# A two-layer decoder trunk on one core: layer 0's rows at a pitch of 2624 bytes, its split weights displaced by chunk, and its matmuls in series of four chunks

## The chip, the core and the metric

The kernel runs on one core of a Trainium2 chip. The metric is the device time of one execution in microseconds (us); before the change it is 2330.52 us, the median of three runs. The core's engines work side by side, each on its own queue of instructions: TensorE (PE: matmuls; PEld: the loads of their weights), VectorE (DVE), ScalarE (ACT), GpSimd (POOL) and SyncE (SP), which issues most transfers from HBM. Semaphores order them where one needs what another made.

## What is computed

The reference is a decoder trunk for one sequence of 256 tokens behind 16 learned ones, with 2048 features, 16 heads of 128 and two layers. Layer 0 has a causal softmax attention with forget gates, layer 1 a stick-breaking attention on keys and values of their own projection; each layer ends in a squared-ReLU MLP of width 8192. Cut to its core:

```python
h = concatenate([meta, x], axis=1)                     # 272 x 2048
for layer in range(2):
    a = rms_norm(h, norm_attn[layer])
    if layer < 1:
        q, k, v, f_logit = split(a @ fox_w_in[0], ...)
        cum_logf = cumsum(log_sigmoid(f_logit + fox_b_f[0]))
        h = h + forgetting_attention(q, k, v, cum_logf) @ fox_w_o[0]
    else:
        k_s, v_s = split(rms_norm(h, kv_norm) @ w_kv, 2)
        q = a @ sb_w_q[0]
        h = h + stick_breaking_attention(q, k_s, v_s) @ sb_w_o[0]
    h = h + square(relu(rms_norm(h, norm_mlp[layer]) @ w_up[layer])) @ w_down[layer]
return rms_norm(h, final_norm)[:, 16:]
```

All of it is in fp32.

## The kernel before

The residual `hT` stays in SBUF, features on the 128 partitions: 16 chunks of 128 features, each with its 272 tokens in a row. Layer 0 works on all 272 tokens, layer 1 on the 256 behind the learned ones, but for its keys and values, which are made from all 272. In the code, `t0` is 0 for work on 272 tokens and 16 (`M`) for work on 256. What the texts call layer 0's shape is every group with `t0` = 0.

**Products in three parts.** A projection in fp32 is made from matmuls of the faster type fp32r. Each factor is split in a high part and a rest: x in x hi and x lo, the weights in whi and wlo. A product is whi·hi + whi·lo + wlo·hi; the fourth is left out. `Split` (the class above `split_chunk`) gives one tile of the pool `xs` in which each of the 16 chunks has a row of 640 floats (`XROW`, 2560 bytes), with hi and lo in the same row. `ROWS` says where in the row each begins, in floats: (48, 368) with 272 tokens, (0, 304) with 256.

**Groups.** `gemm_group` makes 512 output features, four output tiles `accs[m]` of 128 each, from all 2048 input features: 4 `kb` of 4 chunks `kc`, hence 4 × 4 × 4 × 3 = 192 matmuls. There are 96 groups, in the order of the program: 12 for Q, K and V and 4 for the output projection of layer 0, 32 for its MLP (up, then down, in four slices of 2048 hidden features), then 4 for Q, 8 for K and V, 4 for the output projection and 32 for the MLP of layer 1. For each `kb`, SP loads 4 chunks of raw weights in two halves `hf` of 2 chunks each (512 KB a transfer) into `raw` (pool `wraw`, 4 buffers). ScalarE copies a half to `whi` with rounding (L229), VectorE subtracts to get `wlo` (L230); both lie in the pool `wspl`, with 4 buffers of each. A `whi` tile holds the two chunks of its half at a pitch of 576 floats (2304 bytes) with `t0` = 16, where they begin 16 floats (64 bytes) in, and at a pitch of 512 floats (2048 bytes) with `t0` = 0, where they begin at 0.

**Order of the matmuls.** `gemm_matmul` (L182) issues each and, but for the first group, ties it behind the one before, so that TensorE's order in a group is the one that the loops write. `runs` cuts the 48 matmuls of a `kb`: in `kb` 0 and 3 into quarters by output tile (all four chunks for one `m`), in `kb` 1 and 2 into halves by chunk pairs (two chunks for all four `m`). In the first group's `kb` 0 a run is one chunk, as its data are still arriving. Within a run `series` sets the order: with `t0` = 16 first all whi·hi, then all whi·lo, then all wlo·hi; with `t0` = 0 the three of one chunk behind each other.

```python
rows = rows[:, o:o + NC * XROW].rearrange("p (c t) -> p c t", c=NC)
...
    whi = whi.rearrange("p (k c) -> p k c", k=2)[:, :, 16:528]
...
    whi = whi[:, :1024].rearrange("p (k c) -> p k c", k=2)
...
elif kb in (0, 3):
    runs = [(range(4), [m]) for m in range(4)]
else:
    runs = [(range(2 * hf, 2 * hf + 2), range(4)) for hf in range(2)]
```

**What takes up the sums.** When an output tile's last matmul in `kb` 3 is done, `evac` reads it from PSUM on VectorE. In the MLP's up groups that is `relu` (L495), a square on ScalarE, and the split of the result into the next x (`x_u`); in the down groups it is `residual_add` (L259). The attention has matmuls of its own, among them `pta` (L594 to L596) in layer 1. The end of the kernel scales the residual into `ob`, a tile of the pool `xs` as well.

Of the kernel before, what the change touches and what calls it, by code (L numbers as in the profile page):

```python
# [9 lines left out]
F32 = mybir.dt.float32  # L10
F32R = mybir.dt.float32r
# [4 lines left out]
P = 128  # L16
D = 2048
NC = D // P
M = 16
# [6 lines left out]

ROWS = {0: (48, 368), M: (0, 304)}
SPAN = 6
XROW = 640

G_A0, G_M0, G_KV, G_A1, G_M1, G_FIN = range(6)

# [2 lines left out]
def yoco_kernel(ctx: ExitStack, tc: tile.TileContext, hT_in, gains, b_f, w_f, w_qkv0, w_o0, w_up, w_dn,  # L35
                w_kv, w_q1, w_o1, outT):
    nc = tc.nc
# [5 lines left out]
    wspl = ctx.enter_context(tc.tile_pool(name="wspl", bufs=4))  # L43
    xs = ctx.enter_context(tc.tile_pool(name="xs", bufs=2))
# [70 lines left out]
    pad = align.tile([P, 32], F32, name="pad")  # L115
# [3 lines left out]
    class Split:  # L119


        def __init__(self, label, t0):
            n = T - t0
            self.t0 = t0
            rows = xs.tile([P, NC * XROW + 64], F32R, tag="x", name=f"x_{label}")
            hi, lo = ROWS[t0]
            o = min(hi, lo)
            rows = rows[:, o:o + NC * XROW].rearrange("p (c t) -> p c t", c=NC)
            self.hi, self.lo = (rows[:, :, k - o:k - o + n] for k in (hi, lo))

            if t0:
                self.wide = {}
                for name, k in (("hi", hi), ("lo", lo)):
                    nc.gpsimd.tensor_copy(rows[:, 0, k - o + n:k - o + n + SPAN], pad[:, :SPAN])
                    self.wide[name] = rows[:, 0, k - o:k - o + n + SPAN]

    def split_chunk(sp, gi, c):

# [41 lines left out]
    def gemm_matmul(*args, **kw):  # L180

        ins = nc.tensor.matmul(*args, **kw).ins  # L182
        if queued and pinned[0]:
            tc.add_manual_dep(ins, queued[0].name, mybir.DependencyInfo(mybir.DependencyClass.NoSync,
                                                                        mybir.DependencyReason.DATA))
        queued[:] = [ins]

    def gemm_group(wblk, sp, t0, evac, before={}, after={}, load_x=None, widen=False):

        uid[0] += 1
        u = uid[0]
        accs = [pacc.tile([P, 512], F32, tag="acc", name=f"acc_{u}_{m}") for m in range(4)]
        n = T - t0
        for kb in range(4):
            src_w = wblk[kb].rearrange("p (k c) -> p k c", k=4)
            if kb in before:  # L200
                before[kb]()
            piece = 1 if load_x is not None and kb < 2 else 2
            raws = [wraw.tile([P, 2, 512], F32, tag="raw", name=f"raw_{u}_{kb}_{hf}") for hf in range(2)]
            for k0 in range(0, 4, piece):
                if load_x is not None:
                    load_x(range(4 * kb + k0, 4 * kb + k0 + piece))
                if load_x is not None and kb == k0 == 0:

                    for c0 in (0, 256):
                        nc.scalar.dma_start(raws[0][:, 0, c0:c0 + 256], src_w[:, 0, c0:c0 + 256])  # L210
                else:
                    nc.sync.dma_start(raws[k0 // 2][:, k0 % 2:k0 % 2 + piece], src_w[:, k0:k0 + piece])
            parts = []
            for hf in range(2):
                whi = wspl.tile([P, 2 * 576], F32R, tag="whi", name=f"whi_{u}_{kb}_{hf}")
                wlo = wspl.tile([P, 2, 576], F32R, tag="wlo", name=f"wlo_{u}_{kb}_{hf}")
                if t0:
                    whi = whi.rearrange("p (k c) -> p k c", k=2)[:, :, 16:528]
                    wlo = wlo[:, :, 16:528]
                else:  # L220
                    whi = whi[:, :1024].rearrange("p (k c) -> p k c", k=2)
                    wlo = wlo[:, :, :512]
                boxes = [(o, piece, 0, 512) for o in range(0, 2, piece)]
                if load_x is not None and kb == hf == 0:
                    boxes[:1] = [(0, 1, 0, 256), (0, 1, 256, 512)]
                for o, no, c0, c1 in boxes:
                    src = raws[hf][:, o:o + no, c0:c1]
                    hp, lp = whi[:, o:o + no, c0:c1], wlo[:, o:o + no, c0:c1]
                    on_act = nc.scalar.activation(hp, src, AF.Copy)  # L229
                    on_dve = nc.vector.tensor_tensor(out=lp, in0=src, in1=hp.bitcast(F32), op=ALU.subtract)  # L230
                parts.append((whi, wlo))
            if kb in after:
                with tc.issue_after(on_act.ins), tc.issue_after(on_dve.ins):
                    after[kb]()


            if load_x is not None and kb == 0:
                runs = [([kc], range(4)) for kc in range(4)]
            elif kb in (0, 3):
                runs = [(range(4), [m]) for m in range(4)]  # L240
            else:
                runs = [(range(2 * hf, 2 * hf + 2), range(4)) for hf in range(2)]
            pinned[0] = load_x is None
            for kcs, ms in runs:
                if t0:
                    series = [(w, x, kc, m) for w, x in ((0, "hi"), (0, "lo"), (1, "hi")) for m in ms for kc in kcs]
                else:
                    series = [(w, x, kc, m) for m in ms for kc in kcs for w, x in ((0, "hi"), (0, "lo"), (1, "hi"))]
                for i, (w, x, kc, m) in enumerate(series):
                    over = SPAN if widen and kb == m == 0 and i in (0, 4, 8) else 0  # L250
                    rhs = sp.wide[x] if over else getattr(sp, x)[:, 4 * kb + kc]
                    gemm_matmul(accs[m][:, :n + over], parts[kc // 2][w][:, kc % 2, m * P:(m + 1) * P], rhs,
                                start=kb == kc == w == 0 and x == "hi", stop=kb == kc == 3 and w == 1)
                if kb == 3:
                    for m in ms:
                        evac(m, accs[m][:, :n])
# [9 lines left out]
    def load_x(chunks):  # L266
        c0, n = chunks[0], len(chunks)
        nc.sync.dma_start(hT[:, c0:c0 + n, :], hT_in[:, c0:c0 + n, :])
        if c0 == 0:
            nc.sync.dma_start(g_sb, gains)  # L270
        for c in chunks:
            split_chunk(xa, G_A0, c)
# [86 lines left out]
    for g in range(4):  # L359
# [11 lines left out]
        if g == 0:  # L371

            gemm_group(w_qkv0[0], xa, 0, lambda m, acc, qT=qT: nc.scalar.copy(qT[:, m, :], acc),
                       after={kb: (lambda kb=kb: first_norm(kb)) for kb in range(4)}, load_x=load_x)
            gate_products()
            box["rstd"] = norm.finish()
            for m in range(4):
                evac_q(m, qT[:, m, :])
            forget_gates(box["rstd"])
        else:  # L380
            gemm_group(w_qkv0[3 * g], xa, 0, evac_q)
# [4 lines left out]
        def decays(j):  # L386

            for i, (o, n) in enumerate(((0, 144), (144, T))):
                nc.vector.scalar_tensor_tensor(out=s[:, j, o:o + n], in0=fk[:, j, :n],
                                               scalar=fq_sb[:, i, 4 * g + j:4 * g + j + 1],  # L390
                                               in1=maskA[:, o:o + n], op0=ALU.subtract, op1=ALU.add)

        gemm_group(w_qkv0[3 * g + 1], xa, 0, lambda m, acc: evac_kv(m, acc, kT),
                   after={j: (lambda j=j: decays(j)) for j in range(4)})

# [254 lines left out]
    a, y, t, rs = (fin[:, i, :] for i in range(4))  # L650
# [9 lines left out]
    for i in range(2):  # L660
# [2 lines left out]
            nc.tensor.matmul(pr[:, b * P:(b + 1) * P], rs[:, b:b + 1].to_broadcast([P, P]), ident,  # L663
                             start=True, stop=True)
        prs.append(pr[:, :S])
    ob = xs.tile([P, NC * XROW + 64], F32, tag="x", name="ob")[:, :NC * XROW].rearrange("p (c t) -> p c t", c=NC)
    pr_sb = tmp.tile([P, T], F32, tag="relu", name="pr_sb")[:, :S]
    nc.scalar.copy(pr_sb, prs[1])
    for c, n in [(12, 1), (13, 1), (14, 1), (15, 1), (0, 2), (2, 2), (4, 2), (6, 2)]:
# [62 lines left out]
```

## Time and profile before

| | before |
|---|---|
| median of three runs | 2330.52 us (2330.20 to 2330.76) |
| the profiled execution | 2330.78 us |
| its span, first to last instruction | 2329.0 us |
| mean granted clock of TensorE | 0.998 |
| TensorE busy | 2317.9 us, 19,030 matmuls |
| VectorE busy | 1290.1 us |
| ScalarE busy | 1041.3 us |
| HBM read | 407.29 MB, 176 GB/s over the span |

The profile is that of one execution. Busy time is the union of an engine's instructions; matmuls overlap, so that the duration of one (about 0.28 us) is longer than the distance between the starts of two. The chain of waits goes back from the last instruction to what released it, and gives rows of start, length and count. A row of the timeline has the start in the span, the length from the first start to the last end, the engine, the line, the operation with output and inputs, and the count; what stands in brackets is idle time ahead of it and what ended it. A row that groups instructions ends in busy time and mean duration in ns, then the idle time before them.

### The profile page before, as it was taken

Reading aid. Unit: us, or ns where it says so; the run is one execution under the profiler, and the core shown is the slowest. Engines: PE = TensorE matmul, PEld = TensorE weight load, DVE = VectorE, ACT = ScalarE, POOL = GpSimd, SP = SyncE. Lnnn points to the kernel's source line nnn. Section 1 sums busy time; section 2 is a strip of 40 time slices with the busy share of each in tenths; the row PEclk is TensorE's granted clock in tenths of the full one; section 3 lists DMA queues with packets and bytes.
Section 4 is the critical chain, followed back from the end, with each engine's and each line's share of the span. In section 5 each row is a group of like instructions: output and inputs, shape, how many; then the busy total and the mean of one; then the engine's idle time right before and its main releaser. Section 6 shows DMA issues by size and latency. Waiting matters only on the chain.

```text
span 2329.0 us, 44826 instructions
## 1 busy us (share of the span) xinstructions
PE 2317.9 (100%) x19030; PEld 2310.8 (99%) x19030; DVE 1290.1 (55%) x1764; ACT 1041.3 (45%) x1397; POOL 41.6 (2%) x72
## 2 busy tenths in 40 slices
PE   9999999999999999999999999999999999999998
PEld 9999999999999999999999999999999999999998
DVE  7666556554455455455665555566545555555554
ACT  6444344443343344344544444445534443443543
POOL 1000000000000000000000000000000000000000
PEclk9999999999999999999999999999999999999999
DMA  7544545555555555555555444455565655656563
GB/s 235 170 164 157 180 154 168 185 173 181 181 171 183 172 186 176 181 172 183 172 191 181 158 152 151 151 178 186 184 193 180 196 181 185 196 183 191 178 195 127
DMA packets 116904, 412.32 MB, mean 177 GB/s; under 512 B 13520, under 2 KB 16992, under 8 KB 116704
## 3 DMA queue, kind: packets, MB, share of 16 engines
q1 hardware_dynamic: 114560, 406.29, 53.3%
q8 instruction: 149, 2.44, 0.4%
q10 hardware_dynamic: 2144, 3.17, 0.4%
q14 instruction: 51, 0.42, 0.1%
HBM read 407.29 MB, written 2.11 MB: 176 GB/s over the span
## 4 chain that ended last, share of the span: by engine, by line
PE 99%; DMA 1%; DVE 0%; ACT 0%; SPq 0%; issue 0%; DVEq 0%; ACTq 0%
PE acc L182 95%; DMA raw<-w_qkv 1%; PE ps L401 0%; PE pv L334 0%; PE pza L579 0%; PE po L463 0%; PE po L618 0%; PE pzb L580 0%; PE po L619 0%; PE po L464 0%; DVE ob L674 0%; PE pf L301 0%; PE pf L300 0%; PE pta L594 0%; PE pta L595 0%; PE pp L433 0%
## 5 line engine op out<-in xcount | busy, mean ns | idle before, releaser
L230 DVE TENSOR_TENSOR wlo<-raw,whi 128x1024 fp32r<-128x1024 f32 (+1 forms) x773 | 928.6, 1217 | 761.0 <-ACT whi L229 760.5
L229 ACT ACTIVATE whi<-raw 128x1024 fp32r<-128x1024 f32 (+1 forms) x773 | 797.1, 1050 | 1033.7 <-PE acc L182 1010.5
L182 PE MATMUL acc<-x_m,whi 128*128 128x272 f32 (+1 forms) x4096 | 650.8, 283 | 0.0
L182 PE MATMUL acc<-x_u,whi 128*128 128x272 f32 (+1 forms) x4096 | 650.7, 283 | 0.0
L182 PEld LDWEIGHTS acc<-x_m,whi 128*128 128x128 f32 x4096 | 572.3, 188 | 0.1
L182 PEld LDWEIGHTS acc<-x_u,whi 128*128 128x128 f32 x4096 | 572.0, 188 | 0.0
L182 PE MATMUL acc<-x_u,wlo 128*128 128x272 f32 (+1 forms) x2048 | 445.2, 284 | 0.0
L182 PE MATMUL acc<-x_m,wlo 128*128 128x272 f32 (+1 forms) x2048 | 445.2, 284 | 0.0
L182 PE MATMUL acc<-x_a,whi 128*128 128x272 f32 (+1 forms) x2048 | 361.7, 289 | 0.1
L182 PEld LDWEIGHTS acc<-x_u,wlo 128*128 128x128 f32 x2048 | 327.6, 189 | 0.0
L182 PEld LDWEIGHTS acc<-x_m,wlo 128*128 128x128 f32 x2048 | 327.6, 189 | 0.0
L182 PEld LDWEIGHTS acc<-x_a,whi 128*128 128x128 f32 x2048 | 303.2, 189 | 1.2 <-ACT whi L229 0.3
L182 PE MATMUL acc<-x_a,wlo 128*128 128x272 f32 (+1 forms) x1024 | 254.9, 287 | 0.0
L182 PE MATMUL acc<-x_kv,whi 128*128 128x272 f32 x1024 | 191.8, 288 | 0.0
L182 PEld LDWEIGHTS acc<-x_a,wlo 128*128 128x128 f32 x1024 | 176.6, 189 | 1.1 <-issue 0.5
L182 PE MATMUL acc<-x_o,whi 128*128 128x272 f32 (+1 forms) x1024 | 163.7, 284 | 0.0
L182 PEld LDWEIGHTS acc<-x_kv,whi 128*128 128x128 f32 x1024 | 159.7, 188 | 0.0
L182 PE MATMUL acc<-x_kv,wlo 128*128 128x272 f32 x512 | 147.5, 288 | 0.0
L182 PEld LDWEIGHTS acc<-x_o,whi 128*128 128x128 f32 x1024 | 143.2, 188 | 0.0
L259 DVE TENSOR_TENSOR hT<-acc,hT 128x272 f32<-128x272 f32 (+1 forms) x160 | 69.1, 432 | 88.8 <-PE acc L182 87.7
L182 PE MATMUL acc<-x_o,wlo 128*128 128x272 f32 (+1 forms) x512 | 111.6, 284 | 0.0
L182 PEld LDWEIGHTS acc<-x_kv,wlo 128*128 128x128 f32 x512 | 96.5, 188 | 0.0
(225 smaller groups left out, 973.4 us busy)
## 6 DMA issues: line engine op xcount, KB each, us to landing
raw<-w_up SPq DMA_DIRECT2D x256, 512.0 KB, 4.5
raw<-w_dn SPq DMA_DIRECT2D x256, 512.0 KB, 4.4
raw<-w_qkv SPq DMA_DIRECT2D x92, 512.0 KB, 3.8
raw<-w_o SPq DMA_DIRECT2D x64, 512.0 KB, 4.1
raw<-w_kv SPq DMA_DIRECT2D x64, 512.0 KB, 3.8
raw<-w_q SPq DMA_DIRECT2D x32, 512.0 KB, 4.7
fk<-f_dram ACTq DMA_DIRECT2D x4, 544.0 KB, 5.3
raw<-w_qkv SPq DMA_DIRECT2D x7, 256.0 KB, 4.5
```

Of the source, the lines that this page charges most:

```text
L182: ins = nc.tensor.matmul(*args, **kw).ins
L229: on_act = nc.scalar.activation(hp, src, AF.Copy)
L230: on_dve = nc.vector.tensor_tensor(out=lp, in0=src, in1=hp.bitcast(F32), op=ALU.subtract)
L259: nc.vector.tensor_tensor(out=hT[:, c, t0:], in0=acc, in1=hT[:, c, t0:], op=ALU.add)
```

## The change

For work with `t0` = 0, three things change; with `t0` = 16 the offsets in a row and the order stay as they were.

1. The rows of an x tile are 656 floats apart (2624 bytes) instead of 640. The tile itself becomes 16 × 656 floats for all, and begins with the row, without the earlier shift by the smaller offset. The final `ob` keeps rows of 640 floats in the new tile.
2. A weights tile has 1216 floats. With `t0` = 0 its two chunks are 592 floats (2368 bytes) apart, and the second half of a `kb` begins 32 floats (128 bytes) in: the four chunks of a `kb` begin 0, 64, 128 and 192 bytes past a multiple of 256.
3. `kb` 1 and 2 run in quarters by output tile too (in the first group `kb` 2 alone), and the series is the same for both values of `t0`: four chunks of whi·hi, four of whi·lo, four of wlo·hi.

```diff
-XROW = 640
+XROWS = {0: 656, M: 640}
+XTILE = NC * 656
...
-            rows = xs.tile([P, NC * XROW + 64], F32R, tag="x", name=f"x_{label}")
+            rows = xs.tile([P, XTILE], F32R, tag="x", name=f"x_{label}")
             hi, lo = ROWS[t0]
-            o = min(hi, lo)
-            rows = rows[:, o:o + NC * XROW].rearrange("p (c t) -> p c t", c=NC)
-            self.hi, self.lo = (rows[:, :, k - o:k - o + n] for k in (hi, lo))
+            rows = rows[:, :NC * XROWS[t0]].rearrange("p (c t) -> p c t", c=NC)
+            self.hi, self.lo = (rows[:, :, k:k + n] for k in (hi, lo))
...
-                whi = wspl.tile([P, 2 * 576], F32R, tag="whi", name=f"whi_{u}_{kb}_{hf}")
-                wlo = wspl.tile([P, 2, 576], F32R, tag="wlo", name=f"wlo_{u}_{kb}_{hf}")
-                if t0:
-                    whi = whi.rearrange("p (k c) -> p k c", k=2)[:, :, 16:528]
-                    wlo = wlo[:, :, 16:528]
-                else:
-                    whi = whi[:, :1024].rearrange("p (k c) -> p k c", k=2)
-                    wlo = wlo[:, :, :512]
+                whi, wlo = (wspl.tile([P, 1216], F32R, tag=t, name=f"{t}_{u}_{kb}_{hf}") for t in ("whi", "wlo"))
+                o, pitch = (16, 576) if t0 else (32 * hf, 592)
+                whi, wlo = (w[:, o:o + 2 * pitch].rearrange("p (k c) -> p k c", k=2)[:, :, :512] for w in (whi, wlo))
...
-            elif kb in (0, 3):
+            elif kb in (0, 3) or not t0 and (load_x is None or kb == 2):
                 runs = [(range(4), [m]) for m in range(4)]
...
-                if t0:
-                    series = [(w, x, kc, m) for w, x in ((0, "hi"), (0, "lo"), (1, "hi")) for m in ms for kc in kcs]
-                else:
-                    series = [(w, x, kc, m) for m in ms for kc in kcs for w, x in ((0, "hi"), (0, "lo"), (1, "hi"))]
+                series = [(w, x, kc, m) for w, x in ((0, "hi"), (0, "lo"), (1, "hi")) for m in ms for kc in kcs]
...
-    ob = xs.tile([P, NC * XROW + 64], F32, tag="x", name="ob")[:, :NC * XROW].rearrange("p (c t) -> p c t", c=NC)
+    ob = xs.tile([P, XTILE], F32, tag="x", name="ob")[:, :NC * 640].rearrange("p (c t) -> p c t", c=NC)
```

More of the change, by code (lines that the diff above doesn't have):

```diff
@@ L133, in __init__ @@
                 for name, k in (("hi", hi), ("lo", lo)):
-                    nc.gpsimd.tensor_copy(rows[:, 0, k - o + n:k - o + n + SPAN], pad[:, :SPAN])
-                    self.wide[name] = rows[:, 0, k - o:k - o + n + SPAN]
+                    nc.gpsimd.tensor_copy(rows[:, 0, k + n:k + n + SPAN], pad[:, :SPAN])
+                    self.wide[name] = rows[:, 0, k:k + n + SPAN]
     def split_chunk(sp, gi, c):
```

## The prediction

> **What bounds the kernel now.** I read the page's busy times first, then the chain of waits, then single stretches of the timeline.
>
> ```profile
> span 2329.0 us, 44826 instructions
> PE 2317.9 (100%) x19030; PEld 2310.8 (99%) x19030; DVE 1290.1 (55%) x1764; ACT 1041.3 (45%) x1397; POOL 41.6 (2%) x72
> ...
> PEclk9999999999999999999999999999999999999999
> ...
> PE 99%; DMA 1%; DVE 0%; ACT 0%; SPq 0%; issue 0%; DVEq 0%; ACTq 0%
> ```
>
> TensorE is busy for 2317.9 of 2329.0 us at full clock, and the chain that ended last is TensorE for 99 %. So nothing that the other engines do is on the path, as long as their results come in time. What is left is the pace of the matmuls. The profiled execution took 2330.78 us, 1.78 more than its span and 0.26 above the median of the runs shown, 2330.52. I sum against 2330.8.
>
> The chain, in order of time, has two long rows in which TensorE waits for nobody:
>
> ```profile
> 439.88 757.21 PE acc L182 x6144
> 1605.76 705.59 PE acc L182 x6012
> ```
>
> The first lies in layer 0's MLP (272 columns a matmul): 757.21 / 6144 = 123.2 ns each. The second lies in layer 1's (256 columns): 705.59 / 6012 = 117.4 ns. In layer 0 the pace is the same in every group: VectorE takes up the first output tile of one group and the same tile of the next 664.89 − 641.21 = 23.68 us apart, for 192 matmuls, which is 123.3 ns.
>
> ```profile
> 641.21 0.44 DVE L495 SCALAR_TENSOR_TENSOR relu<-acc,rstd_m 128x272 f32<-128x272 f32 x1 [0.69 <-PE acc L182]
> ...
> 664.89 0.44 DVE L495 SCALAR_TENSOR_TENSOR relu<-acc,rstd_m 128x272 f32<-128x272 f32 x1 [0.69 <-PE acc L182]
> ```
>
> **What the pace depends on.** Layer 1 does not run at one pace. These are four stretches of one half of a group there (24 matmuls: eight with whi and x hi, eight with whi and x lo, eight with wlo and x hi), then the first of the next half; columns are start, length and count:
>
> ```profile
> 1802.82 0.96 PE L182 MATMUL acc<-x_m,whi 128*128 128x256 f32 x7
> ...
> 1803.73 1.00 PE L182 MATMUL acc<-x_m,whi 128*128 128x256 f32 x7
> ...
> 1804.68 0.99 PE L182 MATMUL acc<-x_m,wlo 128*128 128x256 f32 x7
> ...
> 1805.62 0.84 PE L182 MATMUL acc<-x_m,whi 128*128 128x256 f32 x6
> ```
>
> The eight with x hi take 1803.73 − 1802.82 = 0.91 us, the first slow one included, and six in the last row take 0.84 us with one duration of 0.28 behind the last start, so 0.56 / 5 = 0.112 us apart: some 113.3 ns, taken between 113.75 and 112. The eight with x lo take 0.95 us, 118.75 ns each. The eight with wlo take 0.94, 117.5 each. Columns, weights tile, engine and clock are the same; what differs is where x lies. From the code, in bytes modulo 256 from the tile's start (whose size is a multiple of 256): layer 1's weights at 64, x hi at 0 and x lo at 304 × 4 = 1216, that is 192. So where the next weights stand 64 bytes ahead of the x that is streaming the pace locks at 113.3, and where they stand 128 away it doesn't. That is my reading of one difference, not a shown cause.
>
> **The change part by part.**
>
> Rows and weights. Before, layer 0's x (hi at 48 × 4 = 192, lo at 368 × 4 = 1472, also 192) is at 192 for every chunk, because the pitch of 2560 bytes is a multiple of 256; weights are at 0. Next weights minus current x: 64. But 272 columns are 1088 bytes, so each stream ends 64 bytes past where it began and the next one jumps back. After, the pitch is 2624, so chunk c begins at 192 + 64c, exactly where the stream of the one before ended; weights of chunk c lie at 64c. Weights and x of one matmul are still 64 apart, but the weights that are loaded while it streams belong to the next chunk: 64(c + 1) − 192 − 64c = −128, that is 128. That the load runs beside the current matmul, not its own, is in the weight loads: the one that belongs to the matmul at 641.38 begins at 641.26, when the one before it begins (641.25).
>
> ```profile
> 641.25 0.28 PE L182 MATMUL acc<-x_m,wlo 128*128 128x272 f32 x1
> 641.38 0.41 PE L182 MATMUL acc<-x_m,whi 128*128 128x272 f32 x2
> ...
> 641.26 0.31 PEld L182 LDWEIGHTS acc<-x_m,whi 128*128 128x128 f32 x2
> ```
>
> So the change gives layer 0 one property of layer 1's fast stretch (a continuous stream) and one of its slow stretch (128). Which decides cannot be read from this trace, as layer 1's stream is continuous in both stretches. Either way it holds for every matmul, since the four chunks close the cycle and hi, lo, whi and wlo have the same offsets.
>
> The count: layer 0's shapes are 56 groups of 192 (12 + 4 + 32 in layer 0 and 8 for K and V), 10,752 matmuls. The first group's kb 0 and 1 keep their runs, 96 matmuls; 10,656 are left.
>
> Price of 16 more columns, from two matmuls of one type that differ in columns only:
>
> ```profile
> L594 PE MATMUL pta<-eh,ntri_r 128*128 128x512 f32 x8 | 3.1, 393 | 0.0
> L596 PE MATMUL pta<-eh,nones_r 128*128 128x288 f32 x8 | 2.4, 296 | 0.0
> ```
>
> (393 − 296) / 224 = 0.433 ns a column, 6.9 ns for 16. At layer 1's slow paces layer 0 would run at 117.5 + 6.9 = 124.4 to 118.75 + 6.9 = 125.65 ns, at its fast pace at 113.3 + 6.9 = 120.2. I take 125.0 for the slow case: + 1.7 × 10,656 = + 18 us. The bounds are the fast pace, − 3.1 × 10,656 = − 33 us, and a slowest one: seven from 1803.73 stand (1.00 − 0.28) / 6 = 120 ns apart, + 6.9 = 126.9, + 3.6 × 10,656 = + 38 us. I choose the slow case because the relation of the load to the stream is what changes between layer 1's two stretches, and here it becomes that of the slow one.
>
> The Trainium skill speaks against any effect at all. In TensorE: Matmul & The Clock Gate, under Step-by-step: what each phase is for, it gives TensorE two independent SBUF read ports, one for the stream and one for the weights, so that a load takes nothing from the running matmul; by that rule the sum would stay at 2330.8 us. This trace's 113.3 against 118.75 ns, with the same shapes, does not fit it.
>
> Order. Quarters by output tile in kb 1 and 2 replace halves by chunk pairs, and a series runs four chunks with one kind of factor instead of the triple of one chunk. The matmuls are the same 192 a group. Layer 1 mixes both run shapes already, within its 117.4 ns. Accumulation in each output tile merely comes in another order. I price this at nothing, as long as the weights come in time.
>
> Weights in time. The cover is the slack of the splits. ScalarE copies whi, VectorE subtracts wlo, each into one of four buffers; SP loads the raw ones.
>
> ```profile
> L230 DVE TENSOR_TENSOR wlo<-raw,whi 128x1024 fp32r<-128x1024 f32 x764 | 922.8, 1224 | 759.0 <-ACT whi L229 758.5
> L229 ACT ACTIVATE whi<-raw 128x1024 fp32r<-128x1024 f32 x764 | 791.9, 1056 | 1031.5 <-PE acc L182 1010.5 <-issue 7.9 <-ACT sq_m L157 6.9
> ...
> 654.02 1.23 DVE L230 TENSOR_TENSOR wlo<-raw,whi 128x1024 fp32r<-128x1024 f32 x1 [1.74 <-ACT whi L229]
> 656.98 1.23 DVE L230 TENSOR_TENSOR wlo<-raw,whi 128x1024 fp32r<-128x1024 f32 x1 [1.73 <-ACT whi L229]
> ...
> raw<-w_up SPq DMA_DIRECT2D x256, 512.0 KB, 4.5
> ```
>
> In kb 1 and 2, half 0's buffers are free after the 24th of 48 matmuls now, and after the 42nd (whi) and 46th (wlo) then: 18 to 22 × 0.123 = 2.2 to 2.7 us later. Half 1 is wanted from the third matmul instead of the 25th, 2.7 us earlier. Both halves of the next-but-one kb are then split one behind the other from the release: 1.06 + 1.22 + 1.22 = 3.5 us until the second wlo stands. TensorE works through the kb between for 48 × 0.123 = 5.92 us, so 2.4 us stay over. Queued behind the waiting copy on ScalarE are the next copy and the output tiles' squares; VectorE's relu rows and their subtractions (four pairs of 0.87 us a group) fit into 5.92 − 2.45. Raw buffers are given back at the same points and the two loads of a kb, 4.5 us to land, have until the kb after the next, 11.8 − 3.5 = 8.3 us. In the first group, where loads set the pace, I allow 0 to 3 us and take nothing. If the cover were gone, each 0.1 us of lateness in the 111 kb blocks (56 × 2 − 1) that change would cost 11 us.
>
> The final output tile `ob` keeps its pitch, and the tiles' sizes (x 41,984 bytes, weights 4,864) stay multiples of 256, so layer 1 is priced at nothing: its 7,680 matmuls keep offsets and order.
>
> Sum: 2330.8 + 18 = 2349 us.
>
> **The rivals.**
>
> *The lock.* What decides is the continuous stream, or the offset of 64 within one matmul. For it: layer 1's fast stretch has both, and layer 0 before has only the second. Against it: the slow stretch with x lo has the continuous stream too, and the weights loading beside it at 128, as here. Time: 2330.8 − 33 = 2298 us. Chance 0.41.
>
> *No effect.* The pace of layer 0 hangs on its columns alone. For it: 123.3 ns stands in every group, whatever the run. Against it: layer 1's two paces. The rule quoted above from the Trainium skill (TensorE: Matmul & The Clock Gate, Step-by-step: what each phase is for) would give this outcome. Time 2331 us. Chance 0.06.
>
> *Late splits.* The releases in bunches make ScalarE's copies wait longer, and half 1's wlo of the next-but-one kb comes after its use. It decides once more than 2.4 us are added to the release chain; 0.2 us beyond it cost 111 × 0.2 = 22 us, hence 2353 us without a change of pace, and TensorE would show idle time ahead of `wlo`. Against it: the 1.7 us of VectorE's idle time in each half. Chance 0.05.
>
> **How the numbers follow.** The slow pace has 0.48, the lock 0.41, no effect 0.06, late splits 0.05. Slower by over 0.2 % (4.7 us, about what a measurement of this kernel tells from no change) is 0.48 + 0.05 = 0.53, faster 0.41, within 0.06. The time is that of the slow pace, 2349 us; its own range is 2342 (117.5 + 6.9 = 124.4, + 1.1 × 10,656 = + 12) to 2362 (a pace of 126.2, between 125.65 and the 126.9 of the slowest row). As the lock holds 0.41, the whole range reaches down to it with 4 us to spare: 2294 to 2362.
>
> **What would show it.** The long row of the chain around 440 to 1197 us gives the pace at once: about 125.0 ns a matmul for the forecast (760 to 772 us for 6144), 120.2 for the lock (739), 123.2 for no effect. The mean durations of layer 0's matmuls, 287 ns before, should rise by a little or fall to near 283. Layer 1's long row stays at 117.4 ns a matmul, or the step that holds it unchanged is wrong. Idle time of TensorE ahead of `whi` or `wlo` in layer 0 would show late splits. A pace that differs between hi and lo, or between whi and wlo, would show that the offsets modulo 256 are not what decides.

## The result, and the profile after

| | before | after |
|---|---|---|
| median of the runs side by side | 2330.64 us (4 runs) | 2358.89 us (2357.71 to 2359.20, 4 runs) |
| ratio of the times | | 1.0117, 95% interval 1.0104 to 1.0129 |
| span of the profiled execution | 2329.0 us | 2357.0 us |

The kernel became slower by 28.2 us. The page of the changed kernel, its first lines and the chain by engine:

```profile
span 2357.0 us, 44844 instructions
PE 2343.7 (99%) x19030; PEld 2337.1 (99%) x19030; DVE 1279.5 (54%) x1764; ACT 1024.5 (43%) x1397; POOL 38.5 (2%) x72
...
PEclk9999999999999999999999999999999999999999
...
PE 99%; DMA 1%; DVE 0%; ACT 0%; SPq 0%; issue 0%; DVEq 0%; ACTq 0%
```

TensorE still sets the end, at full clock, with the same 19,030 matmuls; it is busy for 25.8 us more. The two long rows of the chain of waits (start, length, count) say where:

```profile
449.05 772.33 PE acc L182 x6144
1633.79 705.59 PE acc L182 x6012
```

Layer 0's row grew from 757.21 to 772.33 us, from 123.24 to 125.70 ns a matmul. Layer 1's is 705.59 us in both. The groups by shape show it too: one matmul of 272 columns lasts 289 ns in the mean, and one of 256 columns 280.

```profile
L182 PE MATMUL acc<-x_m,whi 128*128 128x272 f32 x2048 | 299.6, 289 | 0.0
L182 PE MATMUL acc<-x_m,whi 128*128 128x256 f32 x2040 | 271.1, 280 | 0.0
```

In the kernel before the first of these groups stood at 287, and the second had the same row as here:

```profile
L182 PE MATMUL acc<-x_m,whi 128*128 128x272 f32 x2048 | 379.3, 287 | 0.0
```

(The busy time of a group is the union of its matmuls, so it is smaller where they stand in series of four and overlap each other.)

The rest is one wait. In the view of all waits (total, times, longest) the changed kernel has

```profile
ACT whi L224 <- PE acc L182: 1047.7, 408, 5.0
...
PE acc L182 <- ACT whi L224: 2.2, 1, 2.2
```

and the row of the kernel before that stands against the first:

```profile
ACT whi L229 <- PE acc L182: 1010.5, 497, 5.5
```

ScalarE waits for free buffers in 408 places instead of 497, which fits releases in bunches. The last row of the changed kernel is the only wait of a gemm's matmul in that view, once, for 2.2 us, in the first group; before there was none. Together: 10,656 × 2.46 = 26.2 us of pace and 2.2 us of wait make 28.4, against 28.0 measured in the span.

### The profile page after: what moved, and what is told of

It reads as the page before. It is cut to its first block, busy times and chain, and to the rows that moved or that the text cites. A ratio compares the mean times of both kernels' runs of the same rounds, so it can differ in the third digit from the quotient of the medians.

```text
span 2357.0 us, 44844 instructions
## 1 busy us (share of the span) xinstructions
PE 2343.7 (99%) x19030; PEld 2337.1 (99%) x19030; DVE 1279.5 (54%) x1764; ACT 1024.5 (43%) x1397; POOL 38.5 (2%) x72
## 4 chain that ended last, share of the span: by engine, by line
PE 99%; DMA 1%; DVE 0%; ACT 0%; SPq 0%; issue 0%; DVEq 0%; ACTq 0%
PE acc L182 95%; DMA raw<-w_qkv 1%; PE ps L393 0%; PE pv L326 0%; PE pza L571 0%; PE po L455 0%; PE po L610 0%; PE po L611 0%; PE pzb L572 0%; PE po L456 0%; DVE ob L666 0%; PE pf L293 0%; PE pf L292 0%; PE pta L587 0%; PE pta L586 0%; PE pp L425 0%
## 5 line engine op out<-in xcount | busy, mean ns | idle before, releaser
L225 DVE TENSOR_TENSOR wlo<-raw,whi 128x1024 fp32r<-128x1024 f32 (+1 forms) x773 | 919.7, 1216 | 786.5 <-ACT whi L224 785.5
L182 PE MATMUL acc<-x_m,whi 128*128 128x272 f32 (+1 forms) x4096 | 571.2, 284 | 0.0
L182 PE MATMUL acc<-x_u,whi 128*128 128x272 f32 (+1 forms) x4096 | 571.1, 284 | 0.0
L182 PE MATMUL acc<-x_m,wlo 128*128 128x272 f32 (+1 forms) x2048 | 322.4, 285 | 0.0
L182 PE MATMUL acc<-x_u,wlo 128*128 128x272 f32 (+1 forms) x2048 | 322.4, 285 | 0.0
L182 PE MATMUL acc<-x_a,whi 128*128 128x272 f32 (+1 forms) x2048 | 301.6, 289 | 2.2 <-ACT whi L224 2.2
L182 PEld LDWEIGHTS acc<-x_m,wlo 128*128 128x128 f32 x2048 | 279.3, 189 | 0.0
L182 PE MATMUL acc<-x_a,wlo 128*128 128x272 f32 (+1 forms) x1024 | 171.5, 290 | 0.0
L487 DVE SCALAR_TENSOR_TENSOR relu<-acc,rstd_m 128x272 f32<-128x272 f32 (+1 forms) x128 | 54.9, 432 | 60.3 <-PE acc L182 41.7
L182 PE MATMUL acc<-x_kv,wlo 128*128 128x272 f32 x512 | 86.3, 288 | 0.0
L489 ACT ACTIVATE u<-relu 128x272 f32<-128x272 f32 (+1 forms) x128 | 53.2, 418 | 74.3 <-DVE relu L487 74.3
```

The source lines that it names most:

```text
L487: nc.vector.scalar_tensor_tensor(out=r[:, t0:], in0=acc, scalar=0.0, in1=box["r"][:, t0:], op0=ALU.max, op1=ALU.mult)
L489: nc.scalar.activation(u2[:, t0:], r[:, t0:], AF.Square)
```

## The experiments

All times are medians beside runs of the kernel before on the same chip. In what follows the *distance* is where the next matmul's weights begin less where the streaming x begins, modulo 256 bytes; places are *fixed* when they are the same for every chunk and *moving* when they go on by 64 bytes from chunk to chunk. The pace is the chain's long row of layer 0, its MLP, divided by 6144.

### Moving places, three other distances, and the order alone

The change's pitch, weights and order stay; only layer 0's x is put elsewhere in its row.

```diff
-ROWS = {0: (48, 368), M: (0, 304)}
+ROWS = {0: (64, 384), M: (0, 304)}
```

> The changed kernel with layer 0's x 64 bytes further in (hi at float 64, lo at 384): the next weights then stand 64 bytes ahead of the streaming x instead of 128, as in layer 1's fast stretch; weights and x of one matmul stand 0 apart. Load theory (the distance from the streaming x to the weights being loaded sets the pace): the stream locks at about 120.2 ns a matmul, the long row of 6144 takes about 739 us instead of 772, and the time is near 2300 us (2294 to 2306). Order theory (quarters and series cost the time, offsets do not): 2359 us within 5. Pair theory (the distance within one matmul decides): another pace, not 120.2, most likely slow.

Measured 2358.92 us, ratio 1.0118 (1.0103 to 1.0134). Its chain of waits:

```profile
448.47 772.33 PE acc L182 x6144
```

To the hundredth the same row as with distance 128. So the distance 64 does not bring moving places to 120.2 ns, as the load theory expected, and weights and x of one matmul 0 apart give no pace of their own, against the pair theory. The second place:

```diff
+ROWS = {0: (16, 336), M: (0, 304)}
```

> The changed kernel with layer 0's x at float 16 (hi) and 336 (lo): the next weights stand 0 bytes from the streaming x, the weights of the same matmul 192. Load theory: no lock (only the distance 64 has been seen to lock), a pace of 123 to 127 ns and 2330 to 2372 us. Order theory: 2359 us within 5. Pair theory: a pace unlike the other three places.

Measured 2355.84 us, ratio 1.0106 (1.0089 to 1.0123); the row takes 771.32 us, 125.54 ns. The third:

```diff
+ROWS = {0: (32, 352), M: (0, 304)}
```

> The changed kernel with layer 0's x at float 32 (hi) and 352 (lo): the next weights stand 192 bytes from the streaming x, the weights of the same matmul 128. Load theory: no lock, 123 to 127 ns and 2330 to 2372 us. Order theory: 2359 us within 5. Pair theory: as slow as layer 1's stretch with x lo, where weights and x of one matmul are 128 apart too: about 2359 us.

Measured 2341.73 us, ratio 1.0046 (1.0031 to 1.0061). In its chain:

```profile
445.38 760.57 PE acc L182 x6144
```

That is 123.79 ns, 1.9 ns under the changed kernel with nothing changed but a place: offsets change the pace, which the order theory excluded. This gain is one of the MLP. The output projection ahead of it, with the same offsets and the same order, stays at 94.81 / 754 = 125.7 ns:

```profile
350.11 94.81 PE acc L182 x754
```

The order was also tried alone, in the kernel before with all its offsets:

```diff
-            elif kb in (0, 3):
+            elif kb in (0, 3) or not t0 and (load_x is None or kb == 2):
...
+                series = [(w, x, kc, m) for w, x in ((0, "hi"), (0, "lo"), (1, "hi")) for m in ms for kc in kcs]
```

> The kernel before with the change's order alone (quarters in every kb, four chunks in series), all offsets as before: x at 192 for every chunk, weights at 0, so the next weights stand 64 from the streaming x, but each stream jumps back by 64 bytes. Load theory: the time of before, 2331 us within 6, since the distance is that of before at every matmul. Order theory: near the changed kernel's 2359 us.

Measured 2331.99 us, ratio 1.0004 (0.9995 to 1.0013).

```profile
441.55 757.21 PE acc L182 x6144
```

The long row is the 757.21 us of before. It begins 1.67 us later, and the waits of TensorE in the first 60 us have a row for `whi`:

```profile
PE acc L182 <- ACT whi L229: 2.0, 3, 1.2
```

Three waits, 2.0 us in all, are what the trace shows of the order's cost; the time itself is not clear of no change.

### Layer 1 with x lo at x hi's place

```diff
-ROWS = {0: (48, 368), M: (0, 304)}
+ROWS = {0: (48, 368), M: (0, 320)}
```

> The kernel before with layer 1's x lo at float 320 of its row instead of 304, that is at 0 modulo 256 like x hi; layer 0 untouched. Theory that the place of x against the weights sets layer 1's slow stretch: x lo locks like x hi, layer 1's long row of 6012 falls from 705.6 us towards 6012 x 113.4 = 682 us, and the 7,680 matmuls of that shape save up to 31 us: 2300 to 2312 us. Rival, that x lo is slow for another reason (its distance from hi in the row, or its data): the time of before, 2331 us.

Measured 2306.17 us, ratio 0.9893 (0.9879 to 0.9908): this one line beats both kernels. The chain's rows of layer 1's output projection and of its MLP:

```profile
1512.18 89.09 PE acc L182 x785
1601.70 684.54 PE acc L182 x6012
```

And in the timeline, one half of a group of layer 1's MLP:

```profile
1795.02 1.98 PE L182 MATMUL acc<-x_m,whi 128*128 128x256 f32 x16
1796.83 1.07 PE L182 MATMUL acc<-x_m,wlo 128*128 128x256 f32 x8
1797.73 1.52 PE L182 MATMUL acc<-x_m,whi 128*128 128x256 f32 x12
```

Sixteen matmuls with whi, eight with x hi and eight with x lo, begin within 1796.83 − 1795.02 = 1.81 us, 113.1 ns apart, and the eight with wlo within 0.90, 112.5. The slow stretch with x lo is gone, and the slow start of the one behind it too: in the kernel before, the first five of the eight with wlo, which stream x hi, stand 118 to 123 ns apart and only the last three 113 to 114. So the slow stretches hang on the place of x lo, as the prediction read it. Moving x lo changes its distance from the weights and from x hi at once; which of the two counts in layer 1, this run does not tell. The long row falls by 21.05 us.

Not all of layer 1 gains. The row that holds most of its four groups for Q, in the kernel before and here:

```profile
1197.56 106.26 PE acc L182 x894
...
1196.49 106.54 PE acc L182 x894
```

With the same offsets as the MLP, Q runs at 117.8 ns in that row. So the place makes the fast pace possible, but does not ensure it; the last section comes back to this.

### Pitch alone, weights alone

The change has two movements. Each was made without the other, with the change's order:

```diff
-                o, pitch = (16, 576) if t0 else (32 * hf, 592)
+                o, pitch = (16, 576) if t0 else (0, 576)
```

> The changed kernel with layer 0's weights back at 0 for every chunk, only x moves by 64 bytes from chunk to chunk. Now both streams run on without a jump: x because 1088 bytes end where the next chunk begins, the weights because 512 bytes end at a multiple of 256. Before, x jumped and the weights did not; changed, the weights jump and x does not. Theory that jumps of either stream cost: faster than before, towards 120.2 ns a matmul and 2298 us. Theory that a distance that keeps changing cannot lock: 2331 to 2365 us, with a pattern that repeats every four matmuls.

Measured 2349.76 us, ratio 1.0081 (1.0066 to 1.0096).

```profile
446.62 767.30 PE acc L182 x6144
```

Both streams run on without a jump, and the pace is 124.9 ns: a continuous stream does not by itself bring the fast pace. In the trace the distances between starts repeat every four matmuls, 128, 124, 126 and 122 ns, as the second theory expected. The other half:

```diff
-XROWS = {0: 656, M: 640}
+XROWS = {0: 640, M: 640}
```

> The changed kernel with layer 0's row pitch back at 2560 bytes: x at 192 for every chunk, weights at 0, 64, 128, 192. Both streams now jump. Theory that jumps cost: as slow as the changed kernel or slower, 2355 to 2390 us. If the displaced weights alone made the change's loss, about 2359 us; if the pitch alone made it, about 2331 us.

Measured 2363.66 us, ratio 1.0140 (1.0123 to 1.0156).

```profile
449.94 777.38 PE acc L182 x6144
```

So 126.5 ns with moving weights alone, 124.9 with moving x alone, 125.7 with both, and 123.2 with neither: each movement made alone is slower than none, the weights' more, and they do not add up. Where only one side moves, the distance too runs through 0, 64, 128 and 192, so these two runs do not part the movement from the distance. The first experiment does: with the distance at 64 for every matmul, both sides moving, the pace is 125.7.

### Fixed places, four distances and one between

Here nothing moves (pitch 2560, one place for all chunks, the change's order). First x at 128 with weights at 0:

```diff
-ROWS = {0: (48, 368), M: (0, 304)}
+ROWS = {0: (32, 352), M: (0, 304)}
-XROWS = {0: 656, M: 640}
+XROWS = {0: 640, M: 640}
...
-                o, pitch = (16, 576) if t0 else (32 * hf, 592)
+                o, pitch = (16, 576) if t0 else (0, 576)
```

> Pitch 2560 and weights at 0 as before (order of the change), with layer 0's x at 128 instead of 192 (hi at float 32, lo at 352): the next weights stand 128 from the streaming x at every matmul, and nothing moves from chunk to chunk. If the distance decides, as the prediction had it, the pace is that of the changed kernel, 125.7 ns, and the time near 2357 us; if the moving places decide, the time stays near 2331 us.

Measured 2366.88 us, ratio 1.0154 (1.0139 to 1.0169), the slowest of all.

```profile
450.51 777.36 PE acc L182 x6144
```

At fixed places the distance 128 is indeed slow, 126.5 ns. The other four have x at 0 in both layers and differ from each other in one number, the weights' offset `o` (0 in the first, then 48, 16 and 24 floats; layer 1 as in the kernel of 2306 us):

```diff
+ROWS = {0: (0, 320), M: (0, 320)}
+XROWS = {0: 640, M: 640}
...
+                o, pitch = (16, 576) if t0 else (0, 576)
```

> Pitch 2560, the change's order, layer 0's x at 0 for hi and lo and weights at 0: the next weights stand 0 from the streaming x at every matmul, nothing moves from chunk to chunk. Layer 1 has x lo at 0 as well (float 320), which alone gave 2306 us. Theory that a fixed distance sets a pace of its own (64: 123.2 ns, 128: 126.5): a pace other than 123.2 in layer 0's long row of 6144, somewhere in 120 to 127 ns, hence 2272 to 2346 us; no lock is known for 272 columns. Theory that only 128 is slow: 123.2 ns and 2306 us.

Measured 2339.80 us, ratio 1.0035 (1.0022 to 1.0048).

```profile
446.49 777.02 PE acc L182 x6144
```

> As the kernel with distance 0, but layer 0's weights at 192 (float 48): the distance is 192 at every matmul. With moving places 192 was the fastest of the four distances (2342 against 2356 to 2359 us). Theory that a fixed distance sets a pace of its own: near or below 123.2 ns, hence 2290 to 2310 us. Theory that only 128 is slow: 2306 us.

Measured 2344.70 us, ratio 1.0056 (1.0041 to 1.0071); both theories missed.

```profile
449.13 776.99 PE acc L182 x6144
```

> As the kernel with distance 0, but layer 0's weights at 64 (float 16): the distance is 64 as before, with both sides 64 bytes further on than in the kernel before (x 192, weights 0). Theory that the distance decides and not the place itself: layer 0's long row of 6144 takes 757 us as before, 123.2 ns, and the time is 2306 us within 4. If the place itself matters, another pace.

Measured 2311.09 us, ratio 0.9911 (0.9895 to 0.9928).

```profile
440.51 756.88 PE acc L182 x6144
...
1514.08 92.19 PE acc L182 x785
1606.69 684.54 PE acc L182 x6012
```

> As the kernel with the fixed distance of 64, but layer 0's weights at 96 (float 24): a distance of 96, half way between the fast place and 128. Layer 1 as there. Theory that places count in steps of 64 bytes: the pace of one of the neighbours, 123.2 ns and 2311 us or 126.5 ns and 2346 us. Theory that a finer place sets it: another pace, at best a lock at about 120.2 ns, which would give 2311 - 33 = 2278 us.

Measured 2311.15 us, ratio 0.9912 (0.9895 to 0.9928).

```profile
440.76 756.85 PE acc L182 x6144
```

With x untouched, moving the weights alone takes layer 0's long row from 777 to 757 us and back. The distances 0 and 192 are as slow as 128; 64 is fast at both places of the pair that were tried (x 192 and weights 0 before, x 0 and weights 64 here); 96 cannot be told from 64. The time at the shifted 64 is 1.1 us beyond the 4 us that were allowed; the last section shows where that lies. The pace of every place tried, in layer 0's MLP, in ns:

| distance | 0 | 64 | 96 | 128 | 192 |
|---|---|---|---|---|---|
| fixed places | 126.5 | 123.2 | 123.2 | 126.5 | 126.5 |
| moving places | 125.5 | 125.7 | | 125.7 | 123.8 |

The table is one stage. In layer 0's output projection (the row of 754 matmuls ahead of the MLP) fixed 64 and 96 stay at 123.4 and fixed 128 and 192 at 126.7, but fixed 0 runs at 125.4 and moving 192 at 125.7. So the gap between 64 or 96 and the others holds in both stages, while the order among those others does not.

## Why the prediction came out, point by point

**The bound** held. TensorE's pace is the time, and no other engine came into it after the first group.

**Offsets, not order.** Right, and shown: the order alone leaves the row at 757.21 us, while offsets alone, in one and the same order, take it from 757 to 777.

**The slow case.** The forecast chose a pace of 125.0 ns; the row shows 125.70. This term of the sum was too small by 0.7 × 10,656 = 7.5 us of the ten that are missing. The prediction took it midway between layer 1's two slow stretches plus 6.9 ns, and the upper end, 125.65, lies next to what was measured. That is luck. The lower end, 117.5 for the eight with wlo, is no pace of its own but the mean of five matmuls at 118 to 123 ns and three at 113 to 114; by the prediction's own reading these eight have the distance 64 and should have been fast. A fixed distance of 128 runs at 126.5 with 272 columns, not 125.65. And nothing bears out the 6.9 ns: the fastest paces seen are 113.3 with 256 columns and 123.2 with 272, 9.9 apart.

**Its reason** is right for fixed places and does not carry the change. "The relation of the load to the stream is what changes between layer 1's two stretches" was the step, and at fixed places it is so: 64 fast, 128 slow. But the change moves its places, and there the distance 64 gives the same 772.33 us as 128, while 192 is the fastest of the four in the MLP. So the change did not lose by landing on 128 instead of 64; with moving places 64 would have lost as much. It gave up fixed places at the distance 64, which with 96 are the fastest seen with 272 columns, and no moving place that was tried is as fast. That the forecast had the direction right is in this part luck. Why moving places rank their distances otherwise than fixed ones is open.

**The lock at 120.2 ns**, layer 1's fast pace plus the price of 16 columns: no run shows it. At eleven settings of layer 0's offsets beside that of before, the fastest pace is 123.2. The rival of the lock fell with both of its reasons: two continuous streams (124.9) do not bring it, and a distance of 64 in one matmul, which the changed kernel has, does not either. That 272 columns can't reach it is not shown: the code gives layer 1's stages a few wider matmuls at their start, told of in the last section, and layer 0's none. No effect fell with the result.

**The rule quoted against any effect.** The four kernels that differ in the weights' offset alone, at 777.0, 777.0, 756.9 and 756.9 us, show that where the weights lie can slow a series of loads and matmuls by 3.3 ns a matmul. The Trainium skill (TensorE: Matmul & The Clock Gate, Step-by-step: what each phase is for) has loads take nothing from the running matmul, through a port of their own; the outcome that the prediction drew from that rule, no effect, did not come. How the loads slow the series is open. From 500 to 1100 us a load lasts 189 ns in the mean with weights at 0 and 188 at 64, a matmul 291 and 286, which points at the stream rather than the load, but the ends of matmuls in the profile are modelled.

**Weights in time** was right from the second group on: no wait of TensorE on `whi` or `wlo` there, so the slack covered the later release. For the first group the prediction allowed 0 to 3 us and took nothing; it cost 2.2. With the 7.5 above that leaves 0.2 us between the forecast of 2349 and 2358.9. The count of 10,656 leaves out 96 matmuls of the first group whose offsets and order change too; at 2.46 ns each they too are worth 0.2 us.

**Layer 1 at nothing** was right to the hundredth: 705.59 us in both.

## What to carry to other kernels

Where TensorE never waits and still runs the same matmuls at two paces, compare stretches that differ in one thing only; here that showed in the kernel before that x lo's place was slow, and moving it by 64 bytes gave 24 us, while the more elaborate change lost 28. What holds for a place that stays the same need not hold for one that moves from chunk to chunk: try the fixed offsets first, one at a time, and read the pace of the stage in the chain, not the total alone. When only one of two shapes is known to reach a fast pace, its price in columns is no evidence that the other shape can. And read a stretch matmul by matmul before taking its mean for a pace: it can hold two.

## What was not expected of the hardware

The distances 64 and 96 give the same pace, and 128 is slower by 3.3 ns a matmul; where between 96 and 128 the pace changes was not tried.

And the same offsets can run at two paces, within one kernel. In the kernel with x lo at 0 (2306 us), layer 1's MLP runs at 117.8 ns a matmul behind two matmuls of its norm (`pms_m`, at 1601.11 us) and turns to 113.3 at the first of its down groups. The timeline there:

```profile
1679.27 1.10 PE L182 MATMUL acc<-x_m,whi 128*128 128x256 f32 x8
...
1680.68 1.12 PE L182 MATMUL acc<-x_u,whi 128*128 128x262 f32 x8
...
1683.48 1.07 PE L182 MATMUL acc<-x_u,whi 128*128 128x256 f32 x8
...
1684.84 1.07 PE L182 MATMUL acc<-x_u,whi 128*128 128x256 f32 x8
```

Twelve matmuls, the eight of a row and four with wlo, take 1680.68 − 1679.27 = 1.41 us at first and 1684.84 − 1683.48 = 1.36 us behind. At the turn stands a row named by 262 columns. In layer 1 the code gives six more columns to three of the first twelve matmuls for Q, for the output projection and for each up and down half of the MLP (`over = SPAN if widen and kb == m == 0 and i in (0, 4, 8) else 0`). The other four kernels with x lo at 0 turn at the same three matmuls. Where other matmuls come between, the fast pace can be lost: Q runs at 113.3 ns up to two matmuls of its norm (`pms_a`, at 1195.87 us) and at 117.8 behind them. So the fast pace looks entered and left by a series of matmuls, and not set by the offsets alone. No run leaves the wider matmuls out or gives them to layer 0, so that they start it is argued, not shown.

A break can also start it. In the kernel of 2306 us the output projection of layer 1 takes 89.09 us for 785 matmuls, 113.5 ns each; with the fixed distance 64, with the same offsets modulo 256 and the same order in that stage, it takes 92.19 us, 117.4 ns each. Ahead of the attention's last matmuls (`po`) both run at 117.8; behind them the first turns to 113.3 and the second does not. That is 3.1 of the 4.9 us between these two kernels. What decides which pace follows a break is open.
